# Expert gates of a PEER layer: placed in a DRAM matrix by indirect adding transfers of GpSimd, in place of TensorE's products of one-hot matrices

## The chip, the core and the metric

The kernel runs on one core of one Trainium2 chip. The metric is device time in microseconds (us) from launch to end. Five engines work side by side, each through its own list of instructions: TensorE (PE, with its weight loads shown apart as PEld), VectorE (DVE), ScalarE (ACT), GpSimd (POOL) and SyncE (SP), which here only issues transfers. A transfer may be issued from SP, ACT or POOL.

## The reference, cut to what matters

Four layers, each a token mixer and then a PEER layer, on 256 tokens of 1024 numbers. The PEER layer has 16,384 experts, each one row of `u` and one row of `v`. For each token, 8 heads choose 16 experts each by a product of keys, with a softmax over the 16 scores as gates:

```python
s_top, i_top = lax.top_k(sc, 16)                        # per head and key half, of 128
cand = s_top[:, :, 0, :, None] + s_top[:, :, 1, None, :]
cand_idx = i_top[:, :, 0, :, None] * 128 + i_top[:, :, 1, None, :]
best, sel = lax.top_k(cand.reshape(n_tok, 8, 256), 16)
gate = jax.nn.softmax(best, axis=-1)
h = gelu(einsum('cd,ced->ce', tc, u[idx]))              # idx: the 128 chosen experts of a token
y = einsum('ce,ced->cd', gate * h, v[idx])
```

## The kernel before

The kernel does not gather rows of `u` and `v`. It computes all 16,384 experts for all 256 tokens and multiplies with a matrix of gates that is zero where an expert was not chosen. Weights stream in as chunks of 128x1024 (512 KB), 1171 of them for the whole kernel, in the order of `plan`. Each chunk is loaded by SP into one of three buffers `raw` (`_load`, L78), split by ACT into a part `hi` (L88) and by DVE, or now and then by POOL, into the rest `lo` (L94), both in rings of three buffers and two chunks ahead of TensorE (`nxt`, `SPLITAHEAD`). TensorE multiplies hi by the high part of the activations, lo by the high part, hi by the low part.

A PEER layer (`peer`) has these stages:

- 16 chunks of query weights and the scores (`peer_scores`). Beside them DVE runs the search for the best experts (`topk_gen`), a generator that `pace` lets advance by a budget of microseconds for each chunk.
- The u stage: 128 chunks of `u`, chunk j giving 128 experts (`proj_t`, 24 products of 128x256, L121). ACT applies the gelu into `G`, two tiles of 64 chunks (L946, later L941 and L943). The search runs on until chunk 53, then `weights_gen` begins: for 4 tokens at a time DVE builds two one-hot matrices of 128 columns from the indices `tab`, one of them times the gate (L869, L871), TensorE multiplies them into a 128x128 matrix of gates for each token (L885), and ACT or DVE brings the result into `G` (L910, L917, L924).
- The v stage: 128 chunks of `v`. `split_g` splits chunk j+1 of `G` into a high part (ACT, L961) and a low part (DVE, L962) while TensorE multiplies chunk j (`proj_n`, 12 products of 128x512, L131 to L135). Near its end the biases of the next layer are loaded and masked (L1057).

All engines run their instructions in the order in which the program writes them (`manual_schedule`). The two tiles of `G` are also the working memory of the mixers and of the search: the search's arrays lie in `G1`, so it must be over before chunk 64 of the u stage.

Of the kernel before, what the change touches and what calls it, by code (L numbers as in the profile page):

```python
# [10 lines left out]
F32 = mybir.dt.float32  # L11
# [10 lines left out]
T = 256  # L22
# [16 lines left out]
YTAIL = 5  # L39


class Kernel:
# [54 lines left out]

    def nxt(self, ahead=SPLITAHEAD):
# [621 lines left out]
    def peer_scores(self, i):  # L720
# [14 lines left out]
        for hp in range(16):  # L735
            self.xproj(qT[hp % 4])
            if hp % 2 == 0 and hp:
                scores(hp // 2 - 1)
                self.sc_ready = hp - 2
            self.pace(1.3)  # L740
# [3 lines left out]
    def topk_gen(self, tab):  # L744
# [9 lines left out]
        best, ids = self.carve(2, 8, 16), self.carve(128)  # L754
        idi, idj = self.carve(2, 128, dt=I32), self.carve(128, dt=I32)
        stk = self.carve(2, 3, 128)
        den = self.carve(3, 16)

        def top16(vals, idx, src):
            V.max(vals[:, 0:8], src)  # L760
            yield 0.2
            V.max_index(idx[:, 0:8], vals[:, 0:8], src)
            yield 0.2
            V.match_replace(src, vals[:, 0:8], src, LOW)
            yield 0.2
            V.max(vals[:, 8:16], src)
            yield 0.2
            V.max_index(idx[:, 8:16], vals[:, 8:16], src)
            yield 0.2

        for hp in range(16):
            while hp >= self.sc_ready:
                yield 0
            for t in range(2):
                yield from top16(svs[t][:, hp, :], sis[t][:, hp, :], self.sc[:, t, hp, :])
        for t in range(2):
            sv, si = svs[t], sis[t]
            V.tensor_copy(sif, si)
            yield 0.2
# [4 lines left out]
            yield 0.2  # L784
# [4 lines left out]
            yield 0.2  # L789
            V.tensor_copy(sj, f[:, :, 1, :])  # L790
            yield 0.2
            for a, off in enumerate(OFFS):
                if a in (0, 1, 2, 3, 4, 5, 8):
# [5 lines left out]
                    yield 0.2  # L799
            for h in range(8):  # L800
                yield from top16(best[:, t, h, :], pos[:, h, :], cand[:, h, :])
            V.tensor_copy(posf, pos.rearrange("p a b -> p (a b)"))
            yield 0.2
            shape = [128, 4, 16, 16]
            halves = [(slice(h, h + 4), slice(16 * h, 16 * h + 64)) for h in (0, 4)]
            for hs, ks in halves:
# [3 lines left out]
                yield 1.15  # L810
                V.tensor_mul(ge, ge, wa[:, hs][:, :, None, :].to_broadcast(shape))
                yield 1.15
                V.tensor_reduce(ids[:, ks].rearrange("p (h k) -> p h k", h=4), ge, axis=AX.X, op=OP.add)
                yield 1.15
            V.tensor_copy(idi[:, 0, :], ids)
            yield 0.2
            V.tensor_scalar(idi[:, 1, :], idi[:, 0, :], 6, None, op0=OP.logical_shift_right)
            yield 0.2
            V.tensor_scalar(idj, idi[:, 0, :], 63, None, op0=OP.bitwise_and)
            yield 0.2  # L820
            V.tensor_copy(ids, idj)
            yield 0.2
            V.tensor_sub(posf, posf, ids)
            yield 0.2
            for hs, ks in halves:
# [3 lines left out]
                yield 1.15  # L829
                V.tensor_mul(ohb, ohb, sj[:, hs][:, :, None, :].to_broadcast(shape))  # L830
                yield 0.6
                V.tensor_reduce(stk[:, t, 1, ks].rearrange("p (h k) -> p h k", h=4), ohb, axis=AX.X, op=OP.add)
                yield 1.15
            V.tensor_copy(stk[:, t, 0, :], idi[:, 1, :])
            yield 0.2
        b3 = best.rearrange("p t h k -> p (t h) k")
        V.tensor_copy(den[:, 0, :][:, :, None], b3[:, :, 0:1])
        V.tensor_sub(b3, b3, den[:, 0, :][:, :, None].to_broadcast([128, 16, 16]))
        yield 0.2
        nc.scalar.activation(best, best, AF.Exp)  # L840
        yield 0.2
        V.tensor_reduce(den[:, 1, :], b3, axis=AX.X, op=OP.add)
        yield 0.2
        V.reciprocal(den[:, 2, :], den[:, 1, :])
        yield 0.2
        for t in range(2):
            V.tensor_mul(stk[:, t, 2, :].rearrange("p (h k) -> p h k", h=8), best[:, t],
                         den[:, 2, 8 * t:8 * t + 8][:, :, None].to_broadcast([128, 8, 16]))
            yield 0.2
        yield 0  # L850
        yield 0
        for t in range(2):
            p = self.small((128, 4, 128))
            for q in range(3):
                nc.tensor.transpose(p[:, q, :], stk[:, t, q, :], self.ident)
# [356 lines left out]
```

## Time and profile before

| | us |
|---|---|
| median of 3 runs | 3997.79 (3996.78 to 3998.18) |
| the profiled execution | 4000.66 |
| its span, first to last instruction | 3998.8 |
| PE busy | 3934.8 (98%) |
| DVE busy | 3017.9 (75%) |
| ACT busy | 1894.6 (47%) |
| POOL busy | 336.1 (8%) |

The profiled execution's time has 1.9 us more than its span, and is 2.9 us over the median of the runs. TensorE's granted clock is at its higher level nearly throughout (mean 0.997). TensorE's matmuls are pipelined, so the durations of its rows overlap: what a product costs is read from the distance between two starts, not from the duration. The same is true, to a smaller degree, of ACT and DVE: an instruction can start some 0.1 us before the one ahead of it on the engine is shown to end.

### The profile page before, as it was taken

The numbers are of one execution on the slowest core, as the hardware profiler recorded it, in microseconds if no ns is written. First come the engines' busy times: TensorE is split into PE (matmuls) and PEld (weight loads), VectorE is DVE, ScalarE is ACT, GpSimd is POOL, SyncE is SP. The second block draws the span as 40 slices with busy tenths as digits, with TensorE's granted clock in tenths as the row PEclk, the third lists the DMA queues.
The fourth block names the chain that finished last, engine by engine and source line by source line (L and its number), as shares of the span: only waits on it lengthen the run. The fifth ranks groups of instructions, "written<-read, shape, count | busy, mean of one in ns | idle before, by whom it ended". The sixth has DMA issues, their size and how long they took to land. (4 is left out here: it accounts for less than half of the span.)

```text
span 3998.8 us, 68740 instructions
## 1 busy us (share of the span) xinstructions
PE 3934.8 (98%) x26592; PEld 3579.7 (90%) x26592; DVE 3017.9 (75%) x5798; ACT 1894.6 (47%) x3568; POOL 336.1 (8%) x135
## 2 busy tenths in 40 slices
PE   8999999999999999999999999999999999999999
PEld 6999998888998999988887999998888899998887
DVE  7888985566667989965557888985566788996555
ACT  5444444445554444444445444434445444444444
POOL 0111110000001111100000111110000111110000
PEclk9999999999999999999999999999999999999999
DMA  5454445564444554455653554445564455445554
GB/s 182 161 185 151 143 148 187 203 215 156 140 143 143 175 174 143 138 169 189 215 182 105 169 183 152 143 142 187 197 221 148 143 181 168 143 138 175 189 199 159
DMA packets 188007, 668.00 MB, mean 167 GB/s; under 512 B 20688, under 2 KB 27408, under 8 KB 187168
## 3 DMA queue, kind: packets, MB, share of 16 engines
q1 hardware_dynamic: 187424, 663.46, 49.8%
q8 instruction: 209, 3.42, 0.3%
q14 instruction: 118, 0.97, 0.1%
q0 software_dynamic: 64, 0.08, 0.0%
q10 hardware_dynamic: 192, 0.07, 0.0%
HBM read 662.46 MB, written 1.07 MB: 166 GB/s over the span
## 5 line engine op out<-in xcount | busy, mean ns | idle before, releaser
L94 DVE TENSOR_TENSOR lo<-raw,hi 128x1024 fp32r<-128x1024 f32 x1083 | 1324.3, 1223 | 825.4 <-ACT hi L88 821.7
L88 ACT ACTIVATE hi<-raw 128x1024 fp32r<-128x1024 f32 x1212 | 1281.3, 1058 | 724.6 <-PE y L135 696.3
L121 PE MATMUL hp<-zh,hi 128*128 128x256 f32 x5360 | 784.5, 289 | 2.5 <-ACT zh L222 1.7
L121 PE MATMUL hp<-zh,lo 128*128 128x256 f32 x5360 | 752.6, 283 | 0.0
L121 PE MATMUL hp<-zl,hi 128*128 128x256 f32 x5360 | 751.3, 283 | 0.0
L121 PEld LDWEIGHTS hp<-zh,hi 128*128 128x128 f32 x5360 | 689.4, 192 | 9.6 <-issue 4.5
L121 PEld LDWEIGHTS hp<-zh,lo 128*128 128x128 f32 x5360 | 691.7, 192 | 0.0
L121 PEld LDWEIGHTS hp<-zl,hi 128*128 128x128 f32 x5360 | 691.4, 192 | 0.0
L133 PE MATMUL y<-lo,wk 128*128 128x512 f32 x2004 | 632.5, 396 | 0.0
L131 PE MATMUL y<-hi,wk 128*128 128x512 f32 x2004 | 629.0, 394 | 3.5 <-ACT wk L961 3.3
L135 PE MATMUL y<-hi,wk 128*128 128x512 f32 x2004 | 631.8, 396 | 0.2 <-DVE wk L999 0.2
L94 POOL TENSOR_TENSOR lo<-raw,hi 128x1024 fp32r<-128x1024 f32 (+1 forms) x129 | 334.7, 2596 | 3293.6 <-ACT hi L88 3090.5
L131 PEld LDWEIGHTS y<-hi,wk 128*128 128x128 f32 x2004 | 375.7, 188 | 96.6 <-ACT wk L961 4.1
L135 PEld LDWEIGHTS y<-hi,wk 128*128 128x128 f32 x2004 | 376.0, 188 | 93.3 <-DVE wk L999 0.6
L133 PEld LDWEIGHTS y<-lo,wk 128*128 128x128 f32 x2004 | 376.2, 188 | 89.2
L941 ACT ACTIVATE gtmp<-hp 128x256 f32<-128x256 f32 (+52 forms) x284 | 80.6, 284 | 615.3 <-PE hp L121 313.6
L869 DVE TENSOR_TENSOR wk<-iota,tab 128x1024 f32<-128x1024 f32 x256 | 314.1, 1227 | 0.1
L885 PE MATMUL y<-wk 128*128 128x128 f32 x2048 | 271.1, 275 | 13.5 <-DVE wk L871 13.5
L885 PEld LDWEIGHTS y<-wk 128*128 128x128 f32 x2048 | 250.2, 192 | 15.7 <-DVE wk L871 15.7
L871 DVE TENSOR_TENSOR wk<-wk,tab 128x512 f32<-128x512 f32 x256 | 245.7, 960 | 8.8
L946 ACT ACTIVATE G<-hp 128x256 f32<-128x256 f32 x228 | 87.6, 384 | 340.9 <-PE hp L121 340.6
L962 DVE TENSOR_TENSOR wk<-G,wk 128x256 fp32r<-128x256 f32 x492 | 206.0, 419 | 2.4 <-ACT wk L961 2.4
(190 smaller groups left out, 2686.0 us busy)
## 6 DMA issues: line engine op xcount, KB each, us to landing
raw<-in_peer_u SPq DMA_DIRECT2D x512, 512.0 KB, 3.3
raw<-in_peer_v SPq DMA_DIRECT2D x512, 512.0 KB, 3.3
raw<-in_dil_w SPq DMA_DIRECT2D x72, 512.0 KB, 3.6
raw<-in_peer_wq SPq DMA_DIRECT2D x64, 512.0 KB, 3.6
raw<-in_swa_w SPq DMA_DIRECT2D x20, 512.0 KB, 4.0
G<-in_lnp SPq DMA_DIRECT2D x16, 512.0 KB, 4.6
raw<-in_swa_wo SPq DMA_DIRECT2D x16, 512.0 KB, 3.5
G<-relb SPq DMA_DIRECT2D x12, 512.0 KB, 4.7
```

Source lines behind the costliest of these rows:

```text
L88: nc.scalar.activation(h[:, :w], r[:, :w], AF.Copy)
L94: eng.tensor_sub(lo[:, :w], r[:, :w], h.bitcast(F32)[:, :w])
L121: mm(ps, w[:, k, :], z[:, k0 + k, :], start=(p == 0 and k == 0), stop=(p == 2 and k == nk - 1))
L131: mm(ps[t][b][:, :s.stop - s.start], zh[:, ts], hi[:, s], start=first, stop=False)
L133: mm(ps[t][b][:, :s.stop - s.start], zh[:, ts], lo[:, s], start=False, stop=False)
L135: mm(ps[t][b][:, :s.stop - s.start], zl[:, ts], hi[:, s], start=False, stop=last)
L869: V.tensor_tensor(ab, self.iota[:, None, None, :].to_broadcast(shape), tab[:, 0:2, ts][:, :, :, None].to_broadcast(shape), op=OP.is_equal)
L871: V.tensor_mul(ab[:, 1], ab[:, 1], tab[:, 2, ts][:, :, None].to_broadcast([128, 4, 128]))
L885: nc.tensor.matmul(p[:, k, :], ab[:, 0, k, :], ab[:, 1, k, :], start=True, stop=True)
L941: nc.scalar.activation(tmp[:, 0:td], ps[:, 0:td], AF.Gelu)
L946: nc.scalar.activation(g, ps, AF.Gelu)
L962: nc.vector.tensor_sub(gz[:, 1, :], g, gz.bitcast(F32)[:, 0, :])
```

## The change

One-hots, `tab`, `weights_gen` and `keep` are gone. In their place:

- **A matrix in DRAM per layer** (`gates`, 16,384 x 256 numbers, 16.8 MB). It is cleared by 128 transfers of 128 KB from a zero tile, issued by SP within `nxt` (`clear`): two for each chunk from the start of the kernel for the first layer, 0.75 for each chunk from u chunk 64 on for the next layer.
- **The search**, for tokens 0 to 127 first (t = 0), then for 128 to 255 (t = 1). It ends in a place number `ids` and a gate `val` for each of the 128 (head, rank) pairs of a token. The budget of `pace` is 2.0 for each chunk until t = 0 is done, then 1.6. POOL takes 0.4 of the lo splits until t = 0 is done, then none.
- **The scatter**: for each t, 8 heads x 16 ranks, one indirect transfer of POOL that adds 128 gates (one for each token) to 128 places of the matrix. 256 of them for each layer. Two heads of one token may have chosen the same expert, so all 16 transfers of a head wait until the 16 of the head before have landed.
- **The gates are fetched** by SP in the v stage, 128 KB for each chunk, into three buffers `gt` (two of which hold `ids` and `val` before). The first fetch waits for all transfers of the scatter. DVE multiplies the chunk of `G` with it (`gated`) before ACT splits it.

```diff
+    def clear(self, n):
+        while n and self.to_clear:
+            n -= 1
+            self.nc.sync.dma_start(self.to_clear.pop(0), self.zero)
 ...
     def nxt(self, ahead=SPLITAHEAD):
         i = self.n_use
+        self.clear_acc += self.clear_rate
+        while self.clear_acc >= 1:
+            self.clear_acc -= 1
+            self.clear(1)
         self.split_to(i + ahead)
         self.prefetch()
 ...
+    def scatter(self, i, t, ids, val, sent):
+        for h in range(8):
+            mine = f"gates {i} {t} {h}"
+            new = []
+            for k in range(16 * h, 16 * h + 16):
+                ins = self.nc.gpsimd.indirect_dma_start(
+                    self.gates[i], IndirectOffsetOnAxis(ap=ids[:, t, k:k + 1], axis=0), val[:, t, k:k + 1], None,
+                    compute_op=OP.add).ins
 ...
+                for old in sent[t]:
+                    tc.add_manual_dep(ins, old.name, sync, reason="the same token's gates of another head")
 ...
+        def ready(t):
+            if t == 0:
+                self.clear(999)
+            self.pool_share, rate[0] = 0.0, 1.6
+            self.scatter(i, t, ids, val, sent)
 ...
         for j in range(128):
             hi, lo = self.r8(self.nxt())
             ps = self.hps()
             self.proj_t(ps, hi, lo, self.zh, self.zl, 8)
 ...
-            next(late, 0)
-            late = iter(())
-            g = G[j // 64][:, j % 64, :]
-            td = done[1]
-            if td:
-                tmp = self.misc.tile([128, T], F32, name="gtmp", bufs=2)
-                nc.scalar.activation(tmp[:, 0:td], ps[:, 0:td], AF.Gelu)
 ...
+            nc.scalar.activation(G[j // 64][:, j % 64, :], ps, AF.Gelu)
+            if j < 64:
+                self.pace(rate[0])
+            if j == 64 and i + 1 in self.layers:
+                self.next_gates(i + 1)
+                self.clear_rate = 0.75
 ...
+        def fetch(n):
+            while len(gts) < min(n, 128):
+                gt = self.misc.tile([128, T], F32, name="gt", bufs=3)
+                ins = nc.sync.dma_start(gt, rows[len(gts)]).ins
+                if not gts:
 ...
+                    for old in sent[0] + sent[1]:
+                        self.tc.add_manual_dep(ins, old.name, sync, reason="the gates are read")
+                gts.append(gt)
+
+        def gated(j):
+            fetch(j + 3)
+            g = G[j // 64][:, j % 64, :]
+            nc.vector.tensor_mul(g, g, gts[j])
+            return g
 
         def split_g(j):
             gz = self.misc.tile([128, 4, T], F32R, name="wk", bufs=2)
-            g = G[j // 64][:, j % 64, :]
+            g = gated(j)
             nc.scalar.activation(gz[:, 0, :], g, AF.Copy)
             nc.vector.tensor_sub(gz[:, 1, :], g, gz.bitcast(F32)[:, 0, :])
             return gz[:, 0, :], gz[:, 1, :]
```

How the change stands on the engines, at three places. First DVE at the turn from the u stage to the v stage of the first layer, before (the rows L924 are the last products into `G`, L962 the low parts of `G`):

```order
L924 TENSOR_TENSOR G_3644<-G_3644,gtmp 128x256
L94 TENSOR_TENSOR lo<-raw,hi 128x1024
L924 TENSOR_TENSOR G_3644<-G_3644,gtmp 128x256 x2
L962 TENSOR_TENSOR wk<-G_1675,wk 128x256
L94 TENSOR_TENSOR lo<-raw,hi 128x1024
L962 TENSOR_TENSOR wk<-G_1675,wk 128x256
```

In the v stage DVE has two instructions for each chunk. DVE at the same turn in the changed program (L870 writes `val` for t = 1, L97 is the split of L94, L948 the product with the gates, L955 the low part):

```order
L868 RECIPROCAL G_1070<-G_1070 128x8
L870 TENSOR_TENSOR gt<-G_1070 128x128
L97 TENSOR_TENSOR lo<-raw,hi 128x1024 x70
L948 TENSOR_TENSOR G_1728<-G_1728,gt 128x256
L955 TENSOR_TENSOR wk<-G_1728,wk 128x256
L97 TENSOR_TENSOR lo<-raw,hi 128x1024
L948 TENSOR_TENSOR G_1728<-G_1728,gt 128x256
L955 TENSOR_TENSOR wk<-G_1728,wk 128x256
```

The search is over 70 splits before the first product with the gates (38 splits lie between the writes of `val` for t = 0 and t = 1), and in the v stage the product stands between the split of one chunk and the low part of the chunk before it. ACT keeps its order there, hi and then the high part of `G`.

Second POOL in the scatter of the first layer, from the second head on, where before there was a split of `lo` now and then (a DMASW name is a counter of landed POOL transfers; the second head's eight rows with a single wait are cut to three):

```order
L884 DMA gates_140<-gt 4194304x1 [waits DMASW4_49,DMASW5_49,DMASW3_49,DMASW6_49,DMASW2_49,DMASW7_49,DMASW1_49,DMASW0_49]
L884 DMA gates_140<-gt 4194304x1 x7
L884 DMA gates_140<-gt 4194304x1 [waits DMASW2_49]
L884 DMA gates_140<-gt 4194304x1 [waits DMASW3_49]
L884 DMA gates_140<-gt 4194304x1 [waits DMASW4_49]
```

The first transfer of a head waits for all that went before, seven follow without a wait, and each of the last eight waits for the transfer eight places ahead of it.

Third SP at the same turn in the changed program (gates_140 is this layer's matrix, gates_4386 the next layer's):

```order
L105 DMA gates_4386<-zero 128x256
L81 DMA raw<-in_peer_v 128x1024
L938 DMA gt<-gates_140 128x256 x3
L105 DMA gates_4386<-zero 128x256
L81 DMA raw<-in_peer_v 128x1024
L938 DMA gt<-gates_140 128x256
L81 DMA raw<-in_peer_v 128x1024
```

The first fetch, which waits for the scatter, stands behind the load of the fifth `v` chunk and ahead of the sixth.

## Rows read from the trace of the kernel before

**Rows 1.** Page, part 1: busy time, share of the span, instructions

```profile
PE 3934.8 (98%) x26592; PEld 3579.7 (90%) x26592; DVE 3017.9 (75%) x5798; ACT 1894.6 (47%) x3568; POOL 336.1 (8%) x135
```

**Rows 2.** Busy time by stretch, layer 0: late search, v stage, a part of it

```profile
core 0: us, PE busy (x) PEld busy (x) DVE busy (x) ACT busy (x) POOL busy (x), PEclk, DMA share, GB/s
450.00:500.00 50.00, 50.00 (x426) 50.00 (x425) 49.55 (x76) 20.59 (x52) 7.34 (x3) 1.00 0.44 147
582.00:931.00 349.00, 348.17 (x1494) 279.99 (x1493) 210.15 (x265) 172.26 (x252) 0.00 (x0) 1.00 0.59 201
800.00:850.00 50.00, 50.00 (x216) 40.23 (x215) 28.12 (x36) 24.19 (x37) 0.00 (x0) 1.00 0.69 240
```

**Rows 3.** Groups by line: busy us, mean ns, idle before

```profile
L885 PE MATMUL y<-wk 128*128 128x128 f32 x2048 | 271.1, 275 | 13.5 <-DVE wk L871 13.5
L1057 DVE TENSOR_TENSOR G<-G,masks 128x1024 f32<-128x1024 f32 x16 | 19.5, 1218 | 0.0
```

**Rows 4.** Timeline of ACT: first and last gelu of each layer's u stage

```profile
156.11 0.38 ACT L946 ACTIVATE G<-hp 128x256 f32<-128x256 f32 x1
...
158.99 0.38 ACT L946 ACTIVATE G<-hp 128x256 f32<-128x256 f32 x1 [1.55 <-PE hp L121]
...
582.33 0.39 ACT L941 ACTIVATE gtmp<-hp 128x256 f32<-128x256 f32 x1 [1.54 <-issue]
...
1314.24 0.38 ACT L946 ACTIVATE G<-hp 128x256 f32<-128x256 f32 x1
...
1741.76 0.39 ACT L941 ACTIVATE gtmp<-hp 128x256 f32<-128x256 f32 x1 [1.54 <-issue]
...
2263.78 0.38 ACT L946 ACTIVATE G<-hp 128x256 f32<-128x256 f32 x1
...
2693.02 0.39 ACT L941 ACTIVATE gtmp<-hp 128x256 f32<-128x256 f32 x1 [1.59 <-issue]
...
3202.03 0.38 ACT L946 ACTIVATE G<-hp 128x256 f32<-128x256 f32 x1
...
3629.73 0.39 ACT L941 ACTIVATE gtmp<-hp 128x256 f32<-128x256 f32 x1 [1.54 <-issue]
```

**Rows 5.** Timeline of one chunk of the v stage: start, duration, engine

```profile
602.78 0.62 PE L131 MATMUL y<-hi,wk 128*128 128x512 f32 x2
602.98 1.06 ACT L88 ACTIVATE hi<-raw 128x1024 fp32r<-128x1024 f32 x1 [1.43 <-PE y L135]
...
604.07 1.23 DVE L94 TENSOR_TENSOR lo<-raw,hi 128x1024 fp32r<-128x1024 f32 x1 [1.24 <-ACT hi L88]
...
605.21 0.42 DVE L962 TENSOR_TENSOR wk<-G,wk 128x256 fp32r<-128x256 f32 x1
...
605.58 0.62 PE L131 MATMUL y<-hi,wk 128*128 128x512 f32 x2
```

**Rows 6.** Timeline of the turn to the v stage

```profile
582.61 0.41 ACT L961 ACTIVATE wk<-G 128x256 fp32r<-128x256 f32 x1
...
583.07 0.30 PEld L131 LDWEIGHTS y<-hi,wk 128*128 128x128 f32 x2 [1.03 <-ACT wk L961]
583.07 0.73 PE L131 MATMUL y<-hi,wk 128*128 128x512 f32 x2 [0.83 <-ACT wk L961]
```

**Rows 7.** Timeline of POOL's two transfers, then landing times (last number, us)

```profile
1.26 0.68 POOL L1096 DMA_DIRECT2D steps<-in_steps  x1 [0.81 <-POOLq L1205]
1.94 0.54 POOL L1098 DMA_DIRECT2D iota<-in_iota  x1
...
iota<-in_iota POOLq DMA_DIRECT2D x1, 64.0 KB, 5.2
...
relb<-G SPq DMA_DIRECT2D x1, 23.9 KB, 2.1
```

**Rows 8.** Timeline: a POOL split and a DVE product at once

```profile
568.65 2.41 POOL L94 TENSOR_TENSOR lo<-raw,hi 128x1024 fp32r<-128x1024 f32 x1 [17.63 <-ACT hi L88]
568.81 2.52 DVE L924 TENSOR_TENSOR G<-G,gtmp 128x248 f32<-128x248 f32 x1
```

More of the change, by code (lines that the diff above doesn't have):

```diff
@@ L8 @@
 from concourse import mybir
+from concourse.bass import IndirectOffsetOnAxis
 from concourse.bass_utils import run_bass_kernel_spmd
@@ L39 @@
 YTAIL = 5
+ET = mybir.EngineType
+ORDERED = {ET.PE, ET.DVE, ET.Activation, ET.SP}
 class Kernel:
@@ L739, in peer_scores, with topk_gen @@
                 self.sc_ready = hp - 2
-            self.pace(1.3)
+            self.pace(2.0)
         scores(7)
         self.sc_ready = 16
-    def topk_gen(self, tab):
+    def topk_gen(self, ids, val, ready):
         nc = self.nc
@@ L837, in topk_gen @@
[L837 to L848, printed above, removed]
-            yield 0.2
@@ new lines, in topk_gen @@
+            yield 0.28
+            ready(t)
+    def scatter(self, i, t, ids, val, sent):
+        tc = self.tc
+        sync = mybir.DependencyInfo(mybir.DependencyClass.Sync, mybir.DependencyReason.DATA)
+        for h in range(8):
[5 more added lines that the diff above has]
+                    compute_op=OP.add).ins
+                if t:
+                    tc.declare_no_dep(ins, group=f"gates {i} 0", reason="other tokens")
+                if new:
+                    tc.declare_no_dep(ins, group=mine, reason="experts of one head differ")
+                for old in sent[t]:
+                    tc.add_manual_dep(ins, old.name, sync, reason="the same token's gates of another head")
+                tc.add_to_no_dep_group(f"gates {i} {t}", ins)
+                tc.add_to_no_dep_group(mine, ins)
+                new.append(ins)
+            sent[t] = new
@@ L947, in peer @@
-            done[0] = j + 1
-            if self.pace(rate) and not started:
-                started = True
-                self.pool_share = 0.2
-                if G[1] is None:
-                    G[1] = self.big.tile([128, 64, T], F32, name="G1", bufs=1)
-                self.side, self.paced = self.weights_gen(tab, keep), 0.0
-                rate = 67.0 / (125 - j)
-        next(late, 0)
-        self.pace(9999)
+            nc.scalar.activation(G[j // 64][:, j % 64, :], ps, AF.Gelu)
+            if j < 64:
+                self.pace(rate[0])
@@ L996, in peer @@
                 gh, gl = [self.misc.tile([128, 1, T], F32R, name="gtmp", bufs=2) for _ in range(2)]
+            for q in range(m):
+                gated(n + k + q)
             g = G[1][:, 64 - YTAIL + k:64 - YTAIL + k + m, :]
```

185 lines of the change are left out of this document (77 added, 108 removed).

## The prediction

> **What bounds the kernel now.** I read the page's busy shares first: TensorE is busy 98% of the span, at its higher clock level [rows 1, 2]. The longest waits then show that the others wait for it: ACT's splits, for instance, end their idle time when TensorE releases a buffer of `hi` [rows 5]. So a change pays only by TensorE instructions that it removes, and costs by every time TensorE has to wait. I therefore look, stage by stage, at what TensorE does for a chunk, and at how close the chain behind it is.
>
> In the u stage without one-hots two gelus stand 158.99 - 156.11 = 2.88 us apart, the pace of 24 products [rows 4]. In the v stage a chunk takes 605.58 - 602.78 = 2.80 us [rows 5], and TensorE does not stop (348.17 of 349) while DVE is busy for 210 and ACT for 172 [rows 2].
>
> **What the change removes.** From first to last gelu the four u stages take 426.2, 427.5, 429.2 and 427.7 us, together 1710.7 [rows 4]. 127 steps of 2.88 would take 365.8 each, 1463.0 in all. The difference, 247.6 us, is what the one-hot products (2048 records, 512 a layer [rows 3]), the transposes of `tab` and the waits for DVE cost; 61.9 a layer over 512 records is 0.12 us each, the pace of the other small products. All of it lies on TensorE's path, so it goes: -247.6. DVE's builds and products go too, but DVE was hidden there.
>
> **The v stage gets a chain that is too long.** This is the first thing that takes gain back. Before, ACT's high part of `G` waited for nothing but its turn. Now it waits for DVE's product with the gates, and the order on DVE puts that product behind the lo split of another chunk. Follow one turn with the durations of the single chunk and of the turn [rows 5, 6]. TensorE ends chunk j-1; the `hi` split starts 0.20 later (602.98 against 602.78); the lo split follows 1.09 later (604.07), the next DVE instruction 1.14 after that (605.21). That one is now the product: as large as the low part of `G` there, 0.42, and I allow 0.04 until ACT sees it. The high part takes 0.41, TensorE starts 0.05 later (583.07) and the first pair then takes 0.73 instead of 0.62. Sum: 0.20 + 1.09 + 1.14 + 0.46 + 0.41 + 0.05 + 0.11 = 3.46 us from the end of chunk j-1 to the start of chunk j+1. The end of j-1 is its start plus 2.80, so two chunks take at least 6.26, one 3.13 instead of 2.80. 123 chunks of each layer go through the loop: 4 x 123 x 0.33 = +162.
>
> The bounds: the ring on ACT and DVE alone (hi, lo, product, high part, next hi) is 1.09 + 1.14 + 0.46 + 0.31 = 3.00, or +98; with 0.2 for the restart of TensorE instead of 0.11 it is 3.17, or +182. Below zero is excluded, since the product is an extra link. A fetch of 128 KB behind each load is no limit: it is issued two chunks ahead, and the kernel already moves 240 GB/s here with TensorE at 50.00 of 50 [rows 2]; 512 + 128 + 96 KB each 3.13 us are 241 GB/s. DVE's own sum, 1.14 + 0.34 + 0.34, fits.
>
> **The scatter.** POOL issues 256 adding transfers a layer. The time it may take: `val` for t = 0 is written 70 + 38 = 108 splits ahead of the first product with the gates, so 108 u chunks remain, 108 x 2.88 = 311 us; what lies within that is hidden under TensorE. t = 1 is ready after 38 of them (109 us), so POOL never runs dry if t = 0 takes longer than that. What waits for it: SP's first fetch, behind it all later loads of `v` (five chunks are on their way), DVE's first product, and TensorE.
>
> No row shows an indirect adding transfer. POOL's two plain transfers, of 128 rows each, hold it for 0.68 and 0.54 us [rows 7], mean 0.61. An adding one names each place twice, to read and to write, and reads its place numbers: between one and two plain ones, 0.61 to 1.22; I take the middle, 0.92. Landing: a write to DRAM took 2.1 us, a POOL transfer 5.2 at the kernel's start [rows 7]; I take 2.6. Of each head's 16 only the last is waited for in full (8 in flight are 7.4 us of issue, more than 2.6). So a head takes 16 x 0.92 + 2.6 = 17.3, 16 heads 277 us: inside 311, cost 0. With 0.54 it is 180; with 1.22 it is 354, a stall of 43 a layer, +172; at the far end POOL would spend as long as on a split, 2.41 [rows 8], 659 us, and +1390. With 5.2 for landing, 319 at 0.92: +32. All is hidden up to an issue of (311 - 42) / 256 = 1.05 us.
>
> The Trainium skill, "DMA: Bandwidth & Descriptors", section "Anatomy of one DMA — SWDGE (gpsimd) path", puts about 2.0 us of fixed cost on such a transfer, most of it the receipt of the write, and calls the generation of descriptors small. By that rule the issue would stay near those two transfers [rows 7] and the scatter near 200 us, the cost again 0; the trace agrees on plain transfers (0.61 to issue, 2.1 to land for a write), and shows none that adds.
>
> **Small terms.** The turn to the v stage: the first fetch can only go out behind the load of the fifth chunk, about a chunk before TensorE is done, and must land (2.1 to 5.2) and be multiplied: +2 a layer, +8 (0 to 20). The 16 bias additions of 1.22 us on DVE near the end of three v stages [rows 3] now meet a full chain: half of each, +10 (0 to 20). The clears of the first layer, 256 KB a chunk in the swa stage while the first loads run: +5 (0 to 15). The search, at 1.22 + 1.6 = 2.82 us of DVE for a chunk of 2.88: 0, as DVE was at 49.55 of 50 in the late search before and TensorE at 50.00 [rows 2].
>
> Sum on the profiled execution: 4000.7 - 247.6 + 162 + 8 + 10 + 5 = 3938. The median of the runs lies 2.9 lower, so 3935; I give **3930**. With the bounds of these terms, scatter hidden: 3845 to 3985.
>
> **The rivals.**
>
> *The scatter is late (slower).* The gain left is some 70 us, 17 a layer, so the point from which this decides is 311 + 17 = 328 us a layer, an issue of 1.12 us. For it: two addresses for each place could cost the full double, 1.22, and reading the place numbers comes on top. Against: half the estimate's room lies below. At 1.22: 3930 + 172 = 4100. At 1.36, twice the longer row: 390 us, 79 a layer, 4245. At 1.53: 434 us, 4420. TensorE would stand idle ahead of the first `v` chunk of every layer, with SP at the first fetch.
>
> *POOL is held up by DVE.* A POOL split and a DVE product of the same moment took 2.41 and 2.52 us, where such a product takes 0.42 [rows 8, 5]: the two can shut each other out. If each transfer of the 38 busy chunks of t = 1 had to let one DVE instruction of some 0.5 us go first, 109 us would hold 76 transfers instead of 118, and the scatter would end about 42 x 0.92 = 39 us later: 277 + 39 = 316, just past the window, 3950; with an issue of 1.22 it adds the same to the first rival. The Trainium skill, "SBUF — State Buffer", section "SBUF: two separate sides", warns of this: descriptors of POOL's transfers starve while DVE runs copies in its fast modes; its section "Who interferes with whom" exempts products of two tensors, most of DVE's work here. No row of before has a transfer beside DVE's work.
>
> *The v stage keeps its 2.80.* If ACT and DVE ran far enough ahead, the long chain would hide: 3930 - 162 = 3770. Against it: `hi` has three buffers and starts only when TensorE ends a chunk [rows 5], and without that the ring on ACT and DVE alone is 3.00.
>
> **How the numbers follow.** Scatter hidden with the long chain, 3845 to 3985: 0.45. v stage unchanged: 0.03. POOL held up just past the window: 0.04, half of it still faster. Scatter late: 0.48, of which 0.02 is still faster (under 1.10), 0.04 within 0.2%, and 0.42 slower; 0.16 of that lies over 4420. A measurement can tell about 0.2%, 8 us, from no change. Faster 0.45 + 0.03 + 0.02 + 0.02 = 0.52; same 0.04; slower 0.44. The range from 3845 to 4420 leaves out 0.03 below and 0.16 above.
>
> **What the profile will show.** Gelus 2.88 us apart through the whole u stage, and no products of 128x128 but the transposes and scores there. In the v stage ACT's high part of `G` waiting for DVE's product, and a chunk of 3.0 to 3.2 us. POOL's transfers one every 0.6 to 1.05 us, and at the turn a TensorE wait under 5 us; if it is tens of us and ends with a fetch of the gates, the scatter was late. A chunk of 2.80 with the product present would break my chain; an issue over 1.12 breaks the sign.

## The result, and the profile after

The changed kernel takes 5154.76 us (median of 4 runs, 5154.27 to 5156.58), the kernel before 3997.95 in the same comparison: a ratio of 1.2895, 95% interval 1.2873 to 1.2917. The prediction was 3930, range 3845 to 4420: wrong in sign, and the time lies beyond the range. The profiled execution's span is 5153.4 us, 1154.6 more than before. Line numbers below are those of the changed kernel: the splits into `hi` and `lo` are L91 and L97, the u products L141, the v products L151 to L155, the gelu L925, the scatter L884, the fetch of the gates L938, DVE's product with them L948, the high and low part of `G` L954 and L955. Both traces show 1224 loads of weight chunks (the 1171 given above is not the number of either).

The page: busy time (against [rows 1]), TensorE's busy tenths in 40 slices, then four groups (busy us, mean ns, idle time before and what ended most of it).

```profile
PE 3828.9 (74%) x24520; PEld 3321.1 (64%) x24520; DVE 2577.9 (50%) x5125; ACT 1872.3 (36%) x3028; POOL 2114.6 (41%) x1101
...
PE   8999105998999994029999999006999999501998
...
L884 POOL DMA_INDIRECT gates<-gt x1024 | 1934.9, 1890 | 504.9 <-issue 406.9
...
L151 PE MATMUL y<-hi,wk 128*128 128x512 f32 x2004 | 682.5, 421 | 1260.6 <-ACT wk L954 1242.8
...
L954 ACT ACTIVATE wk<-G 128x256 fp32r<-128x256 f32 x492 | 205.2, 417 | 2017.2 <-DVE G L948 2017.2
...
L948 DVE TENSOR_TENSOR G<-G,gt 128x256 f32<-128x256 f32 x512 | 213.5, 418 | 1192.4 <-DMA gt<-gates 1192.3
```

TensorE has less to do than before, by 106 us, and is idle four times: the stretches 105, 402, 006 and 501 among its nines. The three groups below the scatter are links of one chain. TensorE waits for ACT's high part, that for DVE's product, that for a fetch of the gates. The timeline of the first turn (start, duration, then in brackets the idle time before and its releaser) shows what the fetch had waited for:

```profile
828.57 1.55 POOL L884 DMA_INDIRECT gates<-gt  x1 [0.30 <-issue]
831.67 1.28 SPq L938 DMA_DIRECT2D gt<-gates  x3
...
833.66 0.42 DVE L948 TENSOR_TENSOR G<-G,gt 128x256 f32<-128x256 f32 x1 [301.05 <-DMA gt<-gates]
834.12 0.42 ACT L954 ACTIVATE wk<-G 128x256 fp32r<-128x256 f32 x1 [300.84 <-DVE G L948]
...
834.59 1.22 PE L151 MATMUL y<-hi,wk 128*128 128x512 f32 x2 [301.73 <-ACT wk L954]
```

The last transfer of POOL starts at 828.57, the first fetch goes out 3.1 us later, and everything behind it follows at once. It is the first rival of the prediction, the late scatter. From the last gelu to ACT's first high part the four layers take 301, 298, 297 and 292 us, 1188.7 in all, where before 0.28 lay between them [rows 4, 6].

The sum of the difference, from first to last gelu (L925) and first to last high part (L954, before L961) of each layer. Before, the 122 steps of each v stage took 339.6 us, 2 us less than 122 x 2.80, as the first and the last step are shorter:

| | predicted | measured |
|---|---|---|
| u stages | 1463.0 - 1710.7 = -247.6 | 375.8 + 365.8 + 370.9 + 368.1 - 1710.7 = -230 |
| v stages | +162 | 389.7 + 385.0 + 384.7 + 383.4 - 4 x 339.6 = +184 |
| turn and stall of the scatter | +8 and 0 | 1188.7 - 4 x 0.28 = +1188 |
| biases, clears and the rest | +15 | +13, what is left of 1154.6 |

So three of four terms held, and the fourth, put at nothing, is the result. Busy time by stretch of layer 0 (part of the u stage, the stall, part of the v stage) shows the rate of POOL and the granted clock of TensorE, 0.50 (1.2 GHz) in the stall, 1.00 (2.4 GHz) around it:

```profile
core 0: us, PE busy (x) PEld busy (x) DVE busy (x) ACT busy (x) POOL busy (x), PEclk, DMA share, GB/s
...
340.00:440.00 100.00, 100.00 (x836) 100.00 (x835) 42.43 (x35) 46.53 (x70) 81.81 (x34) 1.00 0.80 213
...
540.00:820.00 280.00, 0.00 (x0) 0.00 (x0) 0.00 (x0) 0.00 (x0) 220.94 (x143) 0.50 0.21 0
840.00:1200.00 360.00, 341.36 (x1353) 244.99 (x1352) 236.34 (x350) 160.18 (x225) 0.00 (x0) 1.00 0.77 245
```

POOL starts 34 transfers in 100 us of the u stage, one every 2.9, and 143 in 280 us of the stall, one every 1.96 with the waits between heads. Alone, a transfer lasts 1.55 us and the next starts 0.30 later: 1.855, where the prediction had 0.92. Beside TensorE's work it is slower still, and the timeline of POOL and DVE in the second layer's u stage shows with what it keeps step:

```profile
1799.53 1.22 DVE L97 TENSOR_TENSOR lo<-raw,hi 128x1024 fp32r<-128x1024 f32 x1 [1.66 <-ACT hi L91]
1799.62 2.57 POOL L884 DMA_INDIRECT gates<-gt  x1 [0.30 <-DMA gates<-gt]
1802.41 1.23 DVE L97 TENSOR_TENSOR lo<-raw,hi 128x1024 fp32r<-128x1024 f32 x1 [1.66 <-ACT hi L91]
1802.49 2.57 POOL L884 DMA_INDIRECT gates<-gt  x1 [0.30 <-DMA gates<-gt]
```

Each transfer starts just after DVE's lo split and lasts 2.57 us, 1.02 longer than alone; with the 0.30 that is 2.87, and the next one meets the next split of the chunk of 2.88. About one transfer a chunk, 256 of them against 108 chunks. In the whole trace 372 transfers last over 1.7 us. Each of them started under a DVE instruction with two operands in SBUF, and each ended 1.42 to 1.45 us after that instruction's end. A DVE instruction of the same length with one operand does not do this, as the same layer shows a little earlier (L832 is a sum over one array of the search):

```profile
1763.23 1.21 DVE L832 TENSOR_REDUCE G<-G 128x64 f32<-128x1024 f32 x1
...
1763.33 1.55 POOL L884 DMA_INDIRECT gates<-gt  x1 [0.30 <-issue]
```

All eight transfers that start with over 0.5 us of such a reduction still to come last 1.55.

The theory from this: the stall is the scatter beyond its window of some 300 us (first transfer to last gelu: 300 to 309 us). Its size has two parts, an issue of 1.855 us, and a DVE instruction with two operands in SBUF that shuts out the transfer. The rivals: the turn itself or the fetches are slow; the loads or TensorE, not DVE, slow POOL in the u stage; the v stage is longer for the added traffic and not for the order on DVE.

### The profile page after: what moved, and what is told of

Same layout as the page of the kernel before. It is cut to its first block, busy times and chain, and to the rows that moved or that the text cites. A ratio compares the mean times of both kernels' runs of the same rounds, so it can differ in the third digit from the quotient of the medians.

```text
span 5153.4 us, 65696 instructions
## 1 busy us (share of the span) xinstructions
PE 3828.9 (74%) x24520; PEld 3321.1 (64%) x24520; DVE 2577.9 (50%) x5125; ACT 1872.3 (36%) x3028; POOL 2114.6 (41%) x1101
## 5 line engine op out<-in xcount | busy, mean ns | idle before, releaser
L884 POOL DMA_INDIRECT gates<-gt x1024 | 1934.9, 1890 | 504.9 <-issue 406.9
L97 DVE TENSOR_TENSOR lo<-raw,hi 128x1024 fp32r<-128x1024 f32 x1141 | 1397.6, 1225 | 974.8 <-ACT hi L91 968.2
L151 PE MATMUL y<-hi,wk 128*128 128x512 f32 x2004 | 682.5, 421 | 1260.6 <-ACT wk L954 1242.8
L151 PEld LDWEIGHTS y<-hi,wk 128*128 128x128 f32 x2004 | 340.3, 189 | 1512.7 <-ACT wk L954 1461.3
L91 ACT ACTIVATE hi<-raw 128x1024 fp32r<-128x1024 f32 x1212 | 1273.8, 1052 | 57.1 <-PE y L155 25.0
L97 POOL TENSOR_TENSOR lo<-raw,hi 128x1024 fp32r<-128x1024 f32 (+1 forms) x71 | 178.2, 2513 | 2114.9 <-ACT hi L91 2114.9
L954 ACT ACTIVATE wk<-G 128x256 fp32r<-128x256 f32 x492 | 205.2, 417 | 2017.2 <-DVE G L948 2017.2
L948 DVE TENSOR_TENSOR G<-G,gt 128x256 f32<-128x256 f32 x512 | 213.5, 418 | 1192.4 <-DMA gt<-gates 1192.3
L141 PE MATMUL hp<-zh,hi 128*128 128x256 f32 x5360 | 764.1, 285 | 6.2 <-ACT G L925 3.4
L141 PE MATMUL hp<-zh,lo 128*128 128x256 f32 x5360 | 754.2, 283 | 8.3 <-DVE lo L97 8.3
L141 PE MATMUL hp<-zl,hi 128*128 128x256 f32 x5360 | 753.4, 283 | 0.0
L141 PEld LDWEIGHTS hp<-zh,hi 128*128 128x128 f32 x5360 | 692.1, 192 | 13.5 <-issue 4.5
L141 PEld LDWEIGHTS hp<-zh,lo 128*128 128x128 f32 x5360 | 692.8, 192 | 9.1 <-DVE lo L97 9.1
L141 PEld LDWEIGHTS hp<-zl,hi 128*128 128x128 f32 x5360 | 692.4, 192 | 0.0
L155 PE MATMUL y<-hi,wk 128*128 128x512 f32 x2004 | 626.5, 393 | 0.0
L925 ACT ACTIVATE G<-hp 128x256 f32<-128x256 f32 x512 | 196.6, 384 | 765.6 <-PE hp L141 765.4
L155 PEld LDWEIGHTS y<-hi,wk 128*128 128x128 f32 x2004 | 377.8, 189 | 85.8
L955 DVE TENSOR_TENSOR wk<-G,wk 128x256 fp32r<-128x256 f32 x492 | 209.3, 425 | 267.8 <-ACT wk L954 267.8
L416 ACT ACTIVATE G<-hp 128x256 f32<-128x256 f32 x156 | 59.6, 382 | 204.3 <-PE hp L141 203.4
L336 ACT ACTIVATE G<-G 128x256 f32<-128x256 f32 x96 | 48.2, 502 | 67.3 <-DVE G L328 67.3
```

What stands on the lines that cost most here:

```text
L91: nc.scalar.activation(h[:, :w], r[:, :w], AF.Copy)
L97: eng.tensor_sub(lo[:, :w], r[:, :w], h.bitcast(F32)[:, :w])
L141: mm(ps, w[:, k, :], z[:, k0 + k, :], start=(p == 0 and k == 0), stop=(p == 2 and k == nk - 1))
L151: mm(ps[t][b][:, :s.stop - s.start], zh[:, ts], hi[:, s], start=first, stop=False)
L155: mm(ps[t][b][:, :s.stop - s.start], zl[:, ts], hi[:, s], start=False, stop=last)
L416: self.nc.scalar.activation(dst, ps[:, ::-1] if turned else ps, AF.Copy)
```

## The experiments

**A quarter of the transfers.**

```diff
-            for k in range(16 * h, 16 * h + 16):
+            for k in range(16 * h, 16 * h + 4):
```

> Only the first 4 of each head's 16 adding transfers are made, 64 a layer; the gates of the other ranks are left out, so the output is not the reference's. Theory (the lost time is the scatter beyond its window of some 296 us, and nothing else): 64 transfers, at worst one a chunk of 2.88, take 184 us and end inside the u stage, so the 301, 298, 297 and 292 us that TensorE stands idle at the four turns go: 5154.8 - 1188.6 = 3966 us, with v chunks of 3.1 to 3.2 us as before. Rival 1 (the wait is the turn itself: the first fetch of the gates, its queue or the order of heads): a good part of it stays, over 4100 us. Rival 2 (the idle time also cools TensorE's clock and slows what follows): the v chunks get shorter too, below 3950 us.

Measured 3984.05 us (ratio to before 0.9965, interval 0.995 to 0.998). The stall is gone: the groups of this run show 21 us of DVE's waits for a fetch instead of 1192.

```profile
L884 POOL DMA_INDIRECT gates<-gt x256 | 560.1, 2188 | 343.0 <-DMA gates<-gt 142.1
...
L948 DVE TENSOR_TENSOR G<-G,gt 128x256 f32<-128x256 f32 x512 | 213.5, 418 | 21.5 <-DMA gt<-gates 21.4
```

Against the changed kernel 1170.7 us went, not 1188.6 as expected: between last gelu and first high part 3.8, 5.7, 4.0 and 4.8 us stay, 18 in all, and that is the turn. The v stages are as long as in the changed kernel (383.5 to 389.7 us), so the slow clock of the stall costs nothing after it here, where ACT and DVE are part of the chain and TensorE is not busy throughout. The theory holds, both rivals fall. This is also what the prediction had called "scatter hidden": 3984 where it gave 3935.

**The product one turn earlier.**

```diff
-            g = gated(j)
+            g = G[j // 64][:, j % 64, :]
 ...
             zn = split_g(j + 1) if j < n - 1 else None
+            if j < n - 2:
+                gated(j + 2)
```

> The first 4 of each head's 16 transfers alone, as in the run before, and DVE's product with the gates for chunk j + 2 written behind the low part of chunk j + 1, one turn earlier than in the changed kernel; the gates of the other ranks are left out. Theory (the v stage is longer because the product stands between the lo split and ACT's high part): the high part finds its product done, a v chunk goes back from 3.1 to 3.2 us to 2.80, and 176 us go: 3966 - 176 = 3790 us. Rival (the 128 KB fetch behind every load makes the chunk longer): chunks stay at 3.1 to 3.2 us and the time at 3966 us.

Measured 3787.82 us (3784.33 to 3795.15; ratio to before 0.9479, interval 0.9463 to 0.9495). First the chain in the run before, two chunks of the v stage of its second layer:

```profile
1800.83 1.06 ACT L91 ACTIVATE hi<-raw 128x1024 fp32r<-128x1024 f32 x1
1800.84 0.72 PE L151 MATMUL y<-hi,wk 128*128 128x512 f32 x2
...
1801.93 1.23 DVE L97 TENSOR_TENSOR lo<-raw,hi 128x1024 fp32r<-128x1024 f32 x1 [0.68 <-ACT hi L91]
...
1803.07 0.42 DVE L948 TENSOR_TENSOR G<-G,gt 128x256 f32<-128x256 f32 x1
...
1803.24 0.62 PE L155 MATMUL y<-hi,wk 128*128 128x512 f32 x2
...
1803.58 0.42 ACT L954 ACTIVATE wk<-G 128x256 fp32r<-128x256 f32 x1 [1.69 <-DVE G L948]
1803.90 1.06 ACT L91 ACTIVATE hi<-raw 128x1024 fp32r<-128x1024 f32 x1
...
1804.05 0.73 PE L151 MATMUL y<-hi,wk 128*128 128x512 f32 x2 [0.19 <-ACT wk L954]
...
1806.46 0.62 PE L155 MATMUL y<-hi,wk 128*128 128x512 f32 x2
...
1807.12 0.73 PE L151 MATMUL y<-hi,wk 128*128 128x512 f32 x2
1807.12 1.06 ACT L91 ACTIVATE hi<-raw 128x1024 fp32r<-128x1024 f32 x1
```

From hi to lo 1.10, to the product 1.14, to the high part 0.51, to the next hi 0.32: a ring of 3.07 on ACT and DVE. But the next hi comes 3.22 later. Both start 0.04 us after TensorE's last products of a chunk end (1803.24 + 0.62 and 1806.46 + 0.62), as nearly all of them do. So it is the chain through TensorE that sets the pace: its chunks start 3.21 and 3.07 apart, two in 6.28, where the prediction had 6.26. With the product moved:

```profile
1800.85 1.06 ACT L91 ACTIVATE hi<-raw 128x1024 fp32r<-128x1024 f32 x1 [1.38 <-PE y L155]
...
1801.82 0.40 ACT L954 ACTIVATE wk<-G 128x256 fp32r<-128x256 f32 x1
1801.94 1.23 DVE L97 TENSOR_TENSOR lo<-raw,hi 128x1024 fp32r<-128x1024 f32 x1 [0.85 <-ACT hi L91]
1802.02 0.62 PE L151 MATMUL y<-hi,wk 128*128 128x512 f32 x2
...
1803.42 0.42 DVE L948 TENSOR_TENSOR G<-G,gt 128x256 f32<-128x256 f32 x1
...
1804.77 0.62 PE L151 MATMUL y<-hi,wk 128*128 128x512 f32 x2
```

The high part follows hi without a wait, and ACT waits for TensorE again. A chunk is 2.75 us, the v stages 336.0 to 338.3, shorter than before (339.6); the whole is 196 us less, where 176 was expected since 2.80 had been taken. The fetches cost nothing; the order on DVE was all of it.

**One operand of the lo split out of SBUF.**

```diff
+            if t == 0:
+                self.zp = self.ps.tile([128, 512], F32, name="y0", bufs=1)
+                nc.vector.memset(self.zp, 0.0)
 ...
-        eng.tensor_sub(lo[:, :w], r[:, :w], h.bitcast(F32)[:, :w])
+        if self.zp is not None and w == 1024:
+            eng.tensor_sub(lo.rearrange("p (a b) -> p a b", a=2), r.rearrange("p (a b) -> p a b", a=2),
+                           self.zp[:, None, :].to_broadcast([128, 2, 512]))
+        else:
+            eng.tensor_sub(lo[:, :w], r[:, :w], h.bitcast(F32)[:, :w])
 ...
+        self.zp = None
```

> From the first gates on until the end of the u stage, the lo split of DVE takes its second operand from a PSUM tile of zeros instead of hi in SBUF: same size, same engine, one operand less from SBUF. lo is then the chunk itself, so the output is not the reference's. All 256 transfers a layer are made. Theory (a DVE instruction with two operands from SBUF shuts POOL's transfers out): in the u stage the transfers go from one every 2.3 to 2.9 us to 1.85 apart, as in the idle time at the turn; the scatter takes 256 x 1.855 + 16 x 2 = 507 us instead of some 600, and the stall some 92 us less a layer: 5155 - 370 = 4787 us, up to 4870 where the search's own two-operand instructions still collide. Rival (the traffic of the loads, or TensorE at work, slows the transfers): 2.3 to 2.9 us apart as before, 5155 us.

Measured 4817.86 us, 337 less than the changed kernel. The timeline of POOL and DVE in the second layer's u stage (L99 is the lo split, L889 the scatter):

```profile
1800.77 1.55 POOL L889 DMA_INDIRECT gates<-gt  x1 [0.30 <-issue]
1801.90 1.22 DVE L99 TENSOR_TENSOR lo<-raw,y 128x1024 fp32r<-128x1024 f32 x1 [1.66 <-issue]
1802.62 1.55 POOL L889 DMA_INDIRECT gates<-gt  x1 [0.30 <-issue]
```

The second transfer starts under a split of the same length on the same engine, and lasts 1.55 all the same, with TensorE at work and the loads running as before. So neither of those slows POOL; the second operand in SBUF does. The scatter takes 514 to 520 us a layer instead of 596 to 602, the stall 212 to 216, 855 in all. That is the rest of the trouble: 256 x 1.855 is 475, far over the window with no collision at all. Of the 1189 us at the turns, then, 18 are the turn itself, 837 the issue alone and 333 the hold-up.

**What makes a transfer long.** Four runs change the transfer alone; the last three were timed once each, with the kernel before at 4000.23 us beside them. Without the addition:

```diff
-                    self.gates[i], IndirectOffsetOnAxis(ap=ids[:, t, k:k + 1], axis=0), val[:, t, k:k + 1], None,
-                    compute_op=OP.add).ins
+                    self.gates[i], IndirectOffsetOnAxis(ap=ids[:, t, k:k + 1], axis=0), val[:, t, k:k + 1], None).ins
```

> All 256 indirect transfers a layer, but each writes its 128 gates instead of adding them; where two heads of a token chose the same expert, one gate is lost, so the output can differ a little. Theory A (an adding transfer is long because each place is named twice, to read and to write): its own time falls from 1.55 to between 0.8 and 1.2 us; beside the lo splits still about one a chunk, but the 130 or so transfers of the idle time go 0.35 to 0.75 us faster each, 45 to 100 us a layer: 4750 to 4980 us. Theory B (the long part is reading the place numbers and writing 128 descriptors): 1.55 us unchanged, 5155 us.

With 64 places of 128:

```diff
-                    self.gates[i], IndirectOffsetOnAxis(ap=ids[:, t, k:k + 1], axis=0), val[:, t, k:k + 1], None,
+                    self.gates[i], IndirectOffsetOnAxis(ap=ids[0:64, t, k:k + 1], axis=0), val[0:64, t, k:k + 1], None,
```

> All 256 adding indirect transfers a layer, but each takes only the places of tokens 0 to 63 of its 128 (64 places instead of 128); the gates of the other tokens are left out, so the output is not the reference's. Theory (POOL's time for a transfer is the work on its places, one after another): a transfer alone takes about half of 1.55, 0.8 to 1.0 us; with the 0.30 after it that fits between two lo splits, so the scatter takes 300 to 420 us and the stall falls from some 297 to between 0 and 120 us a layer: 3970 to 4450 us. Rival (a fixed cost of the instruction): 1.55 us again and 5155 us.

Direct, to fixed places, with and without the addition:

```diff
-                ins = self.nc.gpsimd.indirect_dma_start(
-                    self.gates[i], IndirectOffsetOnAxis(ap=ids[:, t, k:k + 1], axis=0), val[:, t, k:k + 1], None,
-                    compute_op=OP.add).ins
+                ins = self.nc.gpsimd.dma_start(
+                    self.gates[i].rearrange("(m s) o -> s m o", m=128)[128 * t + k], val[:, t, k:k + 1],
+                    accum_op=OP.add, allow_slow_non_contiguous=True).ins
```

> The 256 indirect transfers of a layer are replaced by direct ones of POOL that add the same 128 numbers of 4 bytes to 128 fixed places, with the same order and waits; the gates land in wrong places, so the output is not the reference's. By the runs so far an adding indirect transfer costs 1.55 us, a writing indirect one 0.97, a writing direct one 0.54 to 0.68. Theory (the cost is a sum: 0.58 for the addition, 0.36 for the place numbers): 0.97 + 0.58 - 0.36 = 1.19 us alone. Beside the lo splits, theory C (it is the reading of the place numbers from SBUF that the two-operand instruction shuts out): 1.2 us there too, one every 1.5 us, scatter 384 + 30 us, stall some 115 us a layer, about 4430 us. Rival D (it is the writing of the descriptors): transfers wait for the lo split there too, 1.2 to 2.2 us long, one or two in a chunk of 2.88, scatter 450 to 560 us, 4600 to 5000 us.

> The same direct transfers of POOL without the addition; the gates land in wrong places, so the output is not the reference's. Theory (cost as in the kernel before, 0.54 to 0.68 us): with 0.30 between two, 256 x 0.91 + 30 = 263 us, inside the u stage: no stall at the turn, 3970 to 3985 us as with 64 transfers. Rival (writing transfers of POOL, as the run of the writing indirect ones showed, slow the instructions of all engines when they follow each other at 1.3 us or less): the u stage is longer than 366 us again, by up to 200 us a layer, 4000 to 4750 us.

| transfer of POOL | its time, us | until the next | run, us |
|---|---|---|---|
| direct, writing | 0.54 | none | 3989.2 |
| direct, adding | 14.13 / 16 = 0.88 in a row | none | 3984.88 |
| indirect, writing | 0.97 | 0.30 | 4733.71 |
| indirect, adding, 64 places | 1.41 | 0.30 | 4801.99 |
| indirect, adding, 128 places | 1.55 | 0.30 | 5154.76 |

The direct adding ones in their timeline, 16 in a row past the lo splits:

```profile
1601.49 1.23 DVE L97 TENSOR_TENSOR lo<-raw,hi 128x1024 fp32r<-128x1024 f32 x1 [1.65 <-ACT hi L91]
1601.98 14.13 POOL L884 DMA_DIRECT2D gates<-gt  x16 [4.83 <-DMA gates<-gt]
```

Their rows overlap in the trace (a first one lasts 0.85 us, one within the row 2.3 at the median), so their price is the distance between two ends: 0.88, with a lo split between them or without. That is less than the 1.19 expected, so a layer's scatter takes 288 to 293 us and fits. The turns take 3.8 to 5.8 us with all 256 transfers made: the stall comes from their time, not from their number or what they move. They do not wait for DVE at all: rival D (the writing of descriptors is shut out) falls. The direct writing ones, at 0.54, do not either; their run, 3989.2, ends 4 us above what was expected for them, near enough to the 3984 of the two other runs without a stall. What the direct ones lack is the reading of place numbers from SBUF. So theory C stands, though the runs show only that the hold-up goes with the indirect form; that it is the reading is argued from this. The Trainium skill, "SBUF — State Buffer", section "Who interferes with whom", states that rule: a DVE instruction with two inputs from SBUF contends with a GpSimd instruction that reads SBUF, not with one that only writes it. These two runs and the one with PSUM agree with it, at 1.02 us for each lo split met.

The half-size transfers refute the price by places: 64 places less save 0.14 of 1.55 us, so most of it is a cost of the instruction. Their run is 353 us shorter all the same, where 1024 x 0.14 is 143: at 1.71 apart they fall out of step with the splits, and only 54 to 56 of some 144 beside them are held up in a layer, mostly to 2.0 us:

```profile
1802.14 1.41 POOL L884 DMA_INDIRECT gates<-gt  x1 [0.30 <-issue]
1803.37 1.23 DVE L97 TENSOR_TENSOR lo<-raw,hi 128x1024 fp32r<-128x1024 f32 x1 [1.65 <-ACT hi L91]
1803.86 2.02 POOL L884 DMA_INDIRECT gates<-gt  x1 [0.30 <-issue]
```

The writing indirect ones did what theory A said for POOL (0.97 alone, a scatter of 373 to 393 us, no stall at the turn). Beside the lo split they were held up like the adding ones, to 2.02 us at the most, so the hold-up does not belong to the addition. And they did something else that cost more: the u stages took 612, 514, 584 and 512 us. The timeline of TensorE and POOL in the first layer, from 500 us:

```profile
500.13 0.28 PEld L141 LDWEIGHTS hp<-zl,hi 128*128 128x128 f32 x1 [1.11 <-issue]
500.83 0.37 PE L141 MATMUL hp<-zl,hi 128*128 128x256 f32 x1 [1.02 <-issue]
501.04 0.96 POOL L884 DMA_INDIRECT gates<-gt  x1 [0.30 <-issue]
...
502.31 0.97 POOL L884 DMA_INDIRECT gates<-gt  x1 [0.30 <-issue]
...
503.63 0.37 PE L141 MATMUL hp<-zl,hi 128*128 128x256 f32 x1 [2.42 <-issue]
```

Products that go at 0.12 us apart come one in 1.4 to 2.8 us here, waiting for nothing that the profile names, and ACT and DVE stand still with them. From 500 to 606 us 48 products start, with the DMA engines 5% busy, so the amount that is moved is not what slows them. To see whether the scattered places are to blame, the same writing transfers went to the places of the direct ones (timed once):

```diff
+            V.tensor_scalar(row[:, 0:1], self.steps[:, 32:33], 32768.0, float(128 * t), op0=OP.mult, op1=OP.add)
+            V.tensor_scalar(col, self.iota, row[:, 0:1], None, op0=OP.add)
             V.tensor_copy(ids[:, t, :], col)
```

> The run with writing indirect transfers again, but the place numbers are a fixed pattern (place = 32768 x partition + number of the transfer, the places that the direct transfers wrote to) instead of the experts found; the gates land in wrong places, so the output is not the reference's. In that earlier run all engines crept while the transfers went, and the u stages took 612, 514, 584 and 512 us; the direct writing transfers did nothing of the kind. Theory (the scattered places are the cause): u stages of 366 to 377 us, 3980 to 4010 us in all. Rival (the indirect form of a writing transfer is the cause, wherever it writes): 510 to 610 us again, about 4730 us.

Measured 4484.6 us, u stages of 490, 479, 501 and 511: 501 of the 741 us that the creeping had added over the changed kernel's u stages stay, where the direct writing transfers, at 0.54 us and to the same places, added nothing (3989.2). Neither expectation came true: the creeping belongs to the writing indirect form, and the scattered places make some of it. Why, these runs do not settle; it plays no part in the changed kernel, whose u stages run at 2.88 us a chunk.

**Half by scatter, half by one-hots.** A scatter of 128 transfers might fit the window, and the v stage need not be longer. So tokens 128 to 255 go by the scatter, tokens 0 to 127 by the one-hot products of the kernel before, with the product moved (the lines that come back from the kernel before are cut here):

```diff
-        for t in range(2):
+        for t in (1, 0):
 ...
-            for u in range(66):
+            for u in range(34):
 ...
-            nc.vector.tensor_mul(g, g, gts[j])
+            nc.vector.tensor_mul(g[:, 128:T], g[:, 128:T], gts[j])
```

> Both ways of placing gates, the whole computation: tokens 128 to 255 are searched first and go by the scatter (128 transfers a layer, a matrix of 128 columns), tokens 0 to 127 by the one-hot products of the kernel before (32 steps of 4 tokens instead of 64); the product with the fetched gates, 128x128, is written one turn earlier, as in the run with 4 transfers a head. Were the scatter hidden: 3788 + half of 247.6 for the one-hots = 3912 us. Theory (a transfer that meets the lo split lasts 2.57 and with the 0.30 after it 2.87, one a chunk of 2.88): 128 x 2.88 + 16 x 2 = 400 us against a window of some 300; what is left goes at 1.855, some 60 us a layer late: about 4150 us. Rival (the one-hot builds on DVE, with two operands too, shut POOL out for longer): later still, 4250 us and more.

> The run before, but while the scatter goes DVE's lo split is made of two instructions of 512 columns instead of one of 1024. Theory (a transfer is shut out until the instruction under way ends, and slips in ahead of the next): it waits at most 0.62 instead of 1.02 us, 0.62 + 1.55 + 0.30 = 2.47 is less than a chunk, so the transfers fall out of step with it and go at 2.0 to 2.4 us: 128 x 2.2 + 30 = 310 us, about the window: 3912 to 3970 us, faster than both kernels. Rival (DVE's next instruction starts at once and keeps the port, so POOL waits for both halves): as the run before, 4150 us.

```diff
-        eng.tensor_sub(lo[:, :w], r[:, :w], h.bitcast(F32)[:, :w])
+        for s in [slice(0, w)] if not self.halves else [slice(0, w // 2), slice(w // 2, w)]:
+            eng.tensor_sub(lo[:, s], r[:, s], h.bitcast(F32)[:, s])
```

Measured 3890.97 us (3887.19 to 3896.64), ratio to before 0.9735, interval 0.9718 to 0.9751, and 3895.49 with halves (0.974, 0.9724 to 0.9756): the same. Both beat both kernels, by 2.6% the one before. The page of the first of them (L897 is the scatter, L1038 the product with the gates), and the scatter's row of the second:

```profile
PE 3802.1 (98%) x25556; PEld 3469.8 (89%) x25556; DVE 2791.5 (72%) x5885; ACT 1880.6 (48%) x3420; POOL 1196.2 (31%) x589
...
L897 POOL DMA_INDIRECT gates<-gt x512 | 1016.7, 1986 | 276.2 <-issue 195.8
...
L1038 DVE TENSOR_TENSOR G<-G,gt 128x128 f32<-128x128 f32 x512 | 145.1, 284 | 22.6 <-DMA gt<-gates 22.2
```

```profile
L897 POOL DMA_INDIRECT gates<-gt x512 | 877.5, 1714 | 275.4 <-issue 193.9
```

The expectation of 4150 was wrong for two reasons. The scatter takes 312 to 315 us, 2.45 for a transfer, not 2.88. And the window is 332 to 338 us, not some 300, as the remaining one-hots lengthen the u stage to 395 to 405 us. So the scatter ends 20 to 25 us before the first fetch goes out. With builds and products between the splits POOL no longer keeps step with them, as the timeline of the second layer shows:

```profile
1600.03 2.08 POOL L897 DMA_INDIRECT gates<-gt  x1 [0.31 <-issue]
...
1602.42 1.55 POOL L897 DMA_INDIRECT gates<-gt  x1 [0.30 <-issue]
1602.44 1.24 DVE L99 TENSOR_TENSOR lo<-raw,hi 128x1024 fp32r<-128x1024 f32 x1 [1.59 <-ACT hi L92]
```

The transfer that starts 0.02 ahead of the split lasts 1.55, as if alone. The halves do speed POOL up (274 to 284 us a layer, 2.17 for a transfer), as said; but there was nothing left to gain by it.

Two changes are in this gain, half the one-hots and the product moved. The second alone took 194 us off the v stages in the runs above, more than the 107 that the kernel gains. Without it the half would by these numbers come to 4060 to 4090 us, slower than the kernel before; that is an estimate, from v stages of 1543 us against 1342 here and a product of 0.28 instead of 0.42, and was not run.

## Why the prediction was wrong

- **One-hots, -247.6:** right in kind, -230 measured. The u stages run at 2.88 us a chunk, with 0 to 10 us a layer beside it, 17.5 in all, that the step had left out.
- **The chain of the v stage, +162:** right, +184, 2 us over its upper bound of 182. Place and mechanism are those of the rows above, down to the 6.26 for two chunks (6.28 measured), and moving the product took it away. Of the difference 8 us come from those short steps of the stages before.
- **The turn, +8:** 18, inside its bounds. With the scatter out of the way the kernel takes 3984: the terms that were worked out hold to 49 us, at the edge of the range given for that case. With all 256 transfers, in their direct form, it is 3985.
- **The step that failed: "between one and two plain ones, 0.61 to 1.22; I take the middle, 0.92".** The row chosen [rows 7] is of direct transfers, and for a direct adding one the step is right: 0.88. Indirection took 1.55 - 0.88 = 0.67 more, and 0.30 between two that no row of before could show, as only two stood there. That gives 1.855, 475 us a layer with no collision, and a stall of 837 us in all instead of none: the sign was lost here, on a gain put at some 70. "Reading the place numbers comes on top" stood in the rival, with no price.
- **Landing, 2.6 us:** the wait between two heads was 2.3 us at the median in the changed kernel, 2.1 to 5.3 (the first fetch goes out 1.5 to 1.6 after the last transfer's end), no part of the error. But the 2.1 of [rows 7], which the prediction took for the landing of a write of POOL's kind, is a transfer of SP; POOL's own direct ones took 4.8 us to land when they write and 6.6 when they add, at the median of those two runs.
- **The second rival, POOL held up by DVE:** real, and priced at 39 us a layer where the runs show 83 (the stall without it is 333 us less over four layers). Two things went wrong. It took an instruction of 0.5 us, and only for the 38 chunks in which t = 1 is still searched; the lo split of 1.22 stands in all 108, and of some 107 transfers beside them in a layer 91 to 96 were held up. And it cited an exemption of products from the section of the Trainium skill named above, which is for the generation of descriptors alone; the same section's rule for a GpSimd instruction that reads SBUF is the one that fits these runs.
- **The row farthest off was the nearest, in part by luck.** The far end, 2.41 us [rows 8], was left out of the range as extreme. It was the only row with POOL and a two-operand DVE instruction at once. The mean distance between transfers came out at 599 / 256 = 2.34, but as a mix of 2.87 beside the splits, 1.855 in the stall and the waits between heads; that 2.41 lies near it is a coincidence.
- **The chances:** 0.48 for a late scatter was fair; the range's upper edge at an issue of 1.53 was not, since no reason excluded more.

## What to carry to other kernels

Work that is moved off the bottleneck onto an idle engine is free only while (count x issue), with what holds the issue up, fits the window, so that product needs a measured issue of that very form, or a range that reaches to the farthest row. A step put at nothing because it is hidden deserves the widest bound, and when it does not fit, take as much of it as fits: half of this one, with the product moved, gave 2.6%, the whole, without that, lost 29%. Where a new link enters a chain, write its producer a turn ahead of the split that would otherwise stand in front of it.

## What the runs showed of the hardware

- An indirect adding transfer of POOL costs 1.55 us for 128 places and 1.41 for 64, with 0.30 before the next; a direct adding one costs 0.88 in a row, a direct writing one 0.54.
- A DVE instruction with two operands in SBUF that is under way when the indirect transfer starts holds it up to its end (2.57 instead of 1.55, ending 1.42 to 1.45 after it); the same split with one operand in PSUM does not, nor a reduction of the same length with one operand, and direct transfers are not held up.
- Writing indirect transfers at 1.27 us made TensorE's products creep (1.4 to 2.8 us apart instead of 0.12), and the u stages with them; adding ones at 1.855, direct writing ones at 0.54 and direct adding ones at 0.88 did not. The cause is open.
- After some 300 us of idleness at the lower clock level the v stages took 1542.7 us in all, against 1542.6 in the run without the stall.
